# Last steps of a down projection as seven products, and the loads and sums around them moved

## The chip, the cores and the metric

The kernel runs on one core of one Trainium2 chip. The metric is device time in microseconds (us): the median of three runs is 2465.93 us, lowest 2465.27, highest 2466.05. A difference below 0.2% (4.9 us) is taken as no change.

## The reference, cut to what matters

One layer of an encoder: an input projection, two attention branches, an output projection, and then the feed-forward part, where the change lies. Sizes: 512 tokens, width 2048, inner width 5632, everything in float32.

```python
h2 = rmsnorm(x, norm_ffn)
u = h2 @ w_up                                   # 2048 -> 2 * 5632
u = up[:, :-2] * cw[0] + up[:, 1:-1] * cw[1] + up[:, 2:] * cw[2] + conv_b
gate, val = jnp.split(u, 2, axis=-1)
x = x + (jax.nn.silu(gate) * val) @ w_down      # 5632 -> 2048
```

## The kernel before, in words

Every float32 operand is split into two fp32r parts, hi (ScalarE, ACT, rounds it) and lo (VectorE, DVE, takes the rest), and a product is three matmuls: hi·hi, hi·lo, lo·hi.

The weights come in *units*: 256 input rows by 512 output columns. A unit is multiplied by 256 rows of activations of 512 tokens, so it is a two-by-two block product. In `products` this is done in Strassen–Winograd form: seven products, each on one sum or difference of blocks (a *form*), 7 x 2 x 3 = 42 matmuls of 128x256 a unit. In `tiles_by_halves` it is done plainly with eight: 48 such matmuls a unit. Here "seven products" and "plain" mean these two.

A `Product` unit goes through four phases. `load` (queue SP) fetches its four blocks to a tile `f` of seven places (four such tiles). `sums` (DVE) forms the three missing weight sums in `f`, in three additions. `prep` makes hi and lo of all seven forms in two pieces, "a" with four forms (1024 columns) and "b" with three (768): ACT casts to `wh`, DVE subtracts to `wl`. There are two buffers of each piece, so the prep of a unit waits until the unit two before it has been multiplied. Last comes the use on TensorE (PE). `advance` is called after each unit's matmuls and emits, for units ahead: prep of the next but one, sums of the one behind that, and load of the fourth. Some units are *kept*: their sums are made earlier in the program (`fetch`, `add`, `store`, called by `make_early`), kept in DRAM and loaded with the unit, so DVE does nothing for them at use.

When a step of `products` ends, `combine` turns its seven banks of PSUM (of eight) into four blocks. It comes in three pieces `one`, `two`, `three` that are handed to `advance` and stand between the pieces of the prep it emits. A plain step uses four banks and ends in `evac_plain`, four copies on ACT.

The feed-forward part is 22 steps `up(s)` of 8 units, then `down(part, n)`: three parts of the inner width (7, 7 and 8 units), each with four steps n = 0..3 over the output columns. I write (0,3) for part 0, n = 3, and U0, U1, ... for a step's units. Of the twelve, (0,0), (0,3) and (1,3) are plain before (table `PLAIN`). The activations of a part, made by `up` and kept in DRAM as `act`, must be loaded (`load_act`: 8 transfers of 128 KB per unit on SP, to slots of which there are 56) and split (`split_act`: a cast on ACT and a subtraction on DVE per tile) before the part's n = 0. They take the slots of the activations before them as these are used up. `before(i)` and `after(i)` are hooks around unit i of a step.

`keep` and `dma` pin instructions to the order of the code on their engine; a scheduler orders the rest, PE's matmuls among them, within the dependencies. The attention part ahead of the feed-forward part is mostly left to the scheduler.

## Time and profile before

| what | value |
|---|---|
| median of three runs | 2465.93 us |
| span of the profiled execution | 2464.1 us |
| PE busy | 2436.6 us, 99% |
| DVE busy | 1899.6 us, 77% |
| ACT busy | 1283.5 us, 52% |
| DMA | 525.45 MB, mean 213 GB/s |
| loads of kept sums | 88 of 512 KB |

The profiled execution's own time outside its span is not listed; the span is 1.8 us below the median of the runs, and the steps below are parts of the span. PE is busy throughout, so the time is PE's work plus the stretches in which it stands still or runs slowly. The steps can be told apart by counting weight loads: 42 or 48 for each unit, back from the last.

### The profile page before, as it was taken

How to read it: one execution, taken by the hardware profiler on the slowest of the kernel's cores; microseconds unless marked ns; L12 is line 12 of the kernel's file. 1: busy time of each engine (PE TensorE's matmuls, PEld its weight loads, DVE VectorE, ACT ScalarE, POOL GpSimd, SP SyncE). 2: the span in 40 equal slices, each digit the busy share in tenths (PEclk: the TensorE clock that was granted, in tenths of full speed). 3: DMA queues.
4: the chain of work that ended last, by engine and by line, in shares of the span. 5: the costliest groups of instructions: out<-in, count | busy, mean ns of one | idle time of the engine just before them, and what ended most of it. 6: DMA issues, size and time to landing. Idle time of an engine off the chain costs nothing.

```text
span 2464.1 us, 45745 instructions
## 1 busy us (share of the span) xinstructions
PE 2436.6 (99%) x17430; PEld 2276.2 (92%) x17430; DVE 1899.6 (77%) x3003; ACT 1283.5 (52%) x1962; POOL 330.5 (13%) x406
## 2 busy tenths in 40 slices
PE   9999999999999999999999999999999999999998
PEld 7888888888999888888999999999999999999998
DVE  6787667655888656557888888888888878696898
ACT  5354554365644322334666666666666666453633
POOL 1322122301000111111011111110111101000000
PEclk9999999999999999999999999999999999999999
DMA  5766766746655677777588888888888897766754
GB/s 197 257 230 213 234 207 230 238 139 205 197 163 175 200 271 245 237 232 245 166 213 230 224 225 224 218 234 222 224 228 218 234 277 187 218 187 176 221 158 131
DMA packets 340700, 525.45 MB, mean 213 GB/s; under 512 B 30720, under 2 KB 234112, under 8 KB 340480
## 3 DMA queue, kind: packets, MB, share of 16 engines
q1 hardware_dynamic: 254656, 319.68, 41.8%
q0 software_dynamic: 48384, 128.91, 21.8%
q10 hardware_dynamic: 37440, 73.94, 7.8%
q8 instruction: 136, 2.23, 0.4%
q14 instruction: 84, 0.69, 0.1%
HBM read 377.80 MB, written 98.57 MB: 193 GB/s over the span
## 4 chain that ended last, share of the span: by engine, by line
PE 94%; DVE 2%; DMA 1%; ACT 1%; issue 1%; SPq 0%; DVEq 0%; ACTq 0%
PE mm L78 91%; PE tr L78 2%; PE tr L503 1%; PE tr L351 0%; DVE wl L646 0%; DVE s L1076 0%; DMA a<-in_x_t 0%; DMA s<-act 0%; DMA f<-in_w_down 0%; ACT wh L645 0%; DVE u L795 0%; DVE s L687 0%; ACT s L1075 0%; DMA sums<-s 0%; DVE s L620 0%
## 5 line engine op out<-in xcount | busy, mean ns | idle before, releaser
L78 PE MATMUL mm<-s,wh 128*128 128x256 f32 (+1 forms) x9620 | 1725.0, 289 | 6.6 <-ACT wh L645 2.5
L78 PEld LDWEIGHTS mm<-s,wh 128*128 128x128 f32 x9620 | 1437.1, 188 | 48.7 <-ACT wh L645 3.1
L78 PE MATMUL mm<-s,wl 128*128 128x256 f32 (+1 forms) x4810 | 1249.9, 289 | 3.5 <-DVE wl L646 3.5
L78 PEld LDWEIGHTS mm<-s,wl 128*128 128x128 f32 x4810 | 851.0, 188 | 24.7 <-DVE wl L646 4.5
L645 ACT CAST wh<-f 128x1024 fp32r<-128x1024 f32 (+1 forms) x566 | 516.9, 942 | 482.5 <-PE mm L78 331.3
L646 DVE TENSOR_TENSOR wl<-f,wh 128x1024 fp32r<-128x1024 f32 (+1 forms) x566 | 601.8, 1088 | 147.7 <-ACT wh L645 146.3
L78 PE MATMUL mm<-hi,s 128*128 128x512 f32 x896 | 284.9, 394 | 5.7 <-ACT hi L163 5.7
L747 DVE TENSOR_TENSOR wl<-f,wh 128x1024 fp32r<-128x1024 f32 x85 | 104.1, 1224 | 165.4 <-ACT wh L746 159.7
L746 ACT CAST wh<-f 128x1024 fp32r<-128x1024 f32 x85 | 89.4, 1052 | 238.8 <-PE mm L78 207.0
L78 PEld LDWEIGHTS mm<-hi,s 128*128 128x128 f32 x896 | 167.6, 189 | 38.4 <-ACT hi L163 5.7
L163 ACT CAST hi<-raw 128x1024 fp32r<-128x1024 f32 (+1 forms) x97 | 100.9, 1040 | 188.5 <-PE mm L78 153.9
L78 PE MATMUL mm<-s,hi 128*128 128x512 f32 x640 | 195.4, 392 | 2.1 <-ACT o L519 1.6
L164 DVE TENSOR_TENSOR lo<-raw,hi 128x1024 fp32r<-128x1024 f32 (+1 forms) x97 | 117.5, 1211 | 102.8 <-ACT hi L163 98.7
L78 PE MATMUL mm<-lo,s 128*128 128x512 f32 x448 | 176.3, 395 | 0.0
L78 PEld LDWEIGHTS mm<-s,hi 128*128 128x128 f32 x640 | 119.2, 188 | 25.9 <-ACT o L519 1.8
L600 DVE TENSOR_TENSOR f<-f 128x512 f32<-128x512 f32 x195 | 133.5, 685 | 0.0
L1045 POOL DMA_DIRECT2D o<-a x44 | 52.9, 1202 | 557.8 <-ACT a L1044 336.9
L78 PE MATMUL mm<-s,lo 128*128 128x512 f32 x320 | 118.8, 391 | 0.0
L620 DVE TENSOR_TENSOR s<-s 128x256 f32<-128x256 f32 x236 | 93.2, 419 | 17.1 <-DMA s<-in_w_up 15.0
L78 PEld LDWEIGHTS mm<-lo,s 128*128 128x128 f32 x448 | 84.4, 188 | 16.6
L1042 ACT ACTIVATE o<-u,smalls 128x512 f32<-128x512 f32 x88 | 71.2, 809 | 33.3 <-DVE t L677 30.1
L603 DVE TENSOR_TENSOR f<-f 128x256 f32<-128x256 f32 x195 | 83.0, 426 | 6.7
(150 smaller groups left out, 2029.5 us busy)
## 6 DMA issues: line engine op xcount, KB each, us to landing
f<-sums SPq DMA_DIRECT2D x88, 512.0 KB, 5.3
f<-in_w_up SPq DMA_DIRECT2D x176, 256.0 KB, 3.8
o<-a POOLq DMA_DIRECT2D x88, 511.0 KB, 7.4
f<-in_w_up SPq DMA_DIRECT2D x281, 128.0 KB, 3.8
raw<-in_w_in SPq DMA_DIRECT2D x63, 512.0 KB, 4.4
sums<-s ACTq DMA_DIRECT2D x118, 256.0 KB, 4.1
s<-in_w_up POOLq DMA_DIRECT2D x86, 256.0 KB, 5.4
s<-act SPq DMA_DIRECT2D x168, 128.0 KB, 4.2
```

The source lines that it names most:

```text
L78: return nc.tensor.matmul(o, l, r, start=start, stop=stop, skip_group_check=True).ins
L163: nc.scalar.copy(hi[:, c:c + n], self.raw[:, c:c + n])
L164: nc.vector.tensor_tensor(lo[:, c:c + n], self.raw[:, c:c + n], hi[:, c:c + n].bitcast(F32), ALU.subtract)
L600: keep(nc.vector.tensor_tensor(f[:, 3:5], f[:, 2::-2], f[:, 6].unsqueeze(1).to_broadcast([P, 2, 256]), ALU.add))
L603: keep(nc.vector.tensor_tensor(f[:, 5], f[:, 4], f[:, 2], ALU.add))
L620: add = lambda *args: keep(nc.vector.tensor_tensor(*args, ALU.add))
L645: keep(nc.scalar.copy(hi, f))
L646: keep(nc.vector.tensor_tensor(lo, f, hi.bitcast(F32), ALU.subtract))
L746: keep(nc.scalar.copy(hi, self.f))
L747: keep(nc.vector.tensor_tensor(lo, self.f, hi.bitcast(F32), ALU.subtract))
L1042: keep(nc.scalar.activation(self.o[:, m], u[:, m], AF.Identity, bias=cb[:, i:i + 1], scale=cw[:, i, 1:2]))
L1045: keep(nc.gpsimd.dma_start(self.o[:, :, 1:], first[:, :, :S - 1], accum_op=ALU.add))
```

## The change

Five edits.

1. `PLAIN` goes: (0,3) and (1,3) are done with seven products; only (0,0) is plain.
2. The activations of parts 1 and 2 are loaded without block 1 (7 tiles, as in part 2 before), and the loads and splits are spread by two tables over (p,3) and the following n = 0: unit k of the new activations is loaded ahead of turn `LOADS[k]` and split behind turn `SPLITS[k]`, where turn 0 is U0 of (p,3) and turn 7 U0 of the next n = 0. For part 0 the loads in `up(21)` start two units later, and two of them move to (0,0).
3. Which units are kept: in `up(1)` to `up(20)` units 2 and 3 instead of 2, 3, 7; in n = 0 units 0 to 5 instead of 0 and 1; in (0,3) and (1,3) units 4, 5 and 6.
4. The order of the blocks in `f` is turned round, so that the second row block is loaded whole with one transfer (512 contiguous floats a row in `w_in` and `w_down`, two pieces of 256 in `w_up`); a unit that isn't kept takes two transfers instead of three.
5. The three additions of `sums` no longer follow each other: the first stands between the two pieces of the prep, the second behind them, and the third ahead of the next prep.

```diff
-PLAIN = ((0, 0), (0, 3), (1, 3))
+LOADS = 0, 2, 3, 5, 6, 8, 9, 11
+SPLITS = 2, 4, 5, 7, 8, 10, 11, 13
...
     def advance(*between):
-        prep_to(at["use"] + 1, between)
-        for phase, d in (("sums", 2), ("load", 4)):
+        def phase_units(phase, d):
             while at[phase] < len(products_) and products_[at[phase]].ready(phase, at["use"] + d):
-                getattr(products_[at[phase]], phase)()
                 at[phase] += 1
+                yield products_[at[phase] - 1]
+        hooks = [[*carried], [], []]
+        carried.clear()
+        for u in phase_units("sums", 2):
+            run_all(carried)
+            carried.clear()
+            ops = u.sums()
+            for place, op in zip((1, 2), ops):
+                hooks[place].append(op)
+            carried.extend(ops[2:])
+        for place, op in enumerate(between):
+            hooks[place].append(op)
+        prep_to(at["use"] + 1, hooks)
+        for u in phase_units("load", 4):
+            u.load()
         make_early()
...
         def load(self):
             f = self.f = ffn["f"].tile([P, 7, 256], F32, tag="f", name="f", bufs=4)
-            dma(f[:, 0:2], self.w[:, :, 0])
-            dma(f[:, 2], self.w[:, 1, 1])
+            dma(f[:, 0:2], self.w[:, 1])
             if self.made:
+                dma(f[:, 2], self.w[:, 0, 0])
                 dma(f[:, 3:], self.kept)
             else:
-                dma(f[:, 6], self.w[:, 0, 1])
+                dma(f[:, 2:4], self.w[:, 0])
...
-                    f[:, 3:5], f[:, 2::-2], f[:, 6].unsqueeze(1).to_broadcast([P, 2, 256]),
-                    ALU.add))
-                keep(nc.vector.tensor_tensor(f[:, 5], f[:, 4], f[:, 2], ALU.add))
-                keep(nc.vector.tensor_tensor(f[:, 6], f[:, 5], f[:, 1], ALU.add))
+            return [
+                lambda: add(f[:, 4:2:-1], f[:, 2:0:-1],
+                            f[:, 3].unsqueeze(1).to_broadcast([P, 2, 256])),
+                lambda: add(f[:, 5], f[:, 4], f[:, 1]),
+                lambda: add(f[:, 6], f[:, 5], f[:, 0])]
...
-            blocks = (0, 2, 7, 5, 4, 6, 3, 1)[:8 - (part == 2)]
+            blocks = (0, 2, 7, 5, 4, 6, 3, 1)[:8 - (part > 0)]
...
             if s == pairs_ff - 1:
-                load_act(0, i - 1)
+                load_act(0, i - 3)
...
-                 before=before, after=after, kept=(2, 3, 7) if s else range(8))
+                 before=before, after=after,
+                 kept={0: range(8), pairs_ff - 1: (2, 3, 7)}.get(s, (2, 3)))
...
+        def on_turn(work, turns, i):
+            turn = i if n else i + len(parts[part - 1])
+            if turn in turns and part + (n == 3) < 3:
+                work(part + (n == 3), turns.index(turn))
+
         def before(i):
-            if n == 0 and part:
-                load_act(part, 6 + i)
+            if n == part == 0:
+                load_act(0, 5 + i)
+            elif n in (0, 3):
+                on_turn(load_act, LOADS, i)
...
-            if part < 2 and n == 3:
-                load_act(part + 1, i - 1)
...
         def after(i):
-            if n == 0:
-                split_act(part, i + (5 if part else 2))
-            if part < 2 and n == 3:
-                split_act(part + 1, i - 2)
+            if n == part == 0:
+                split_act(0, i + 2)
+            elif n in (0, 3):
+                on_turn(split_act, SPLITS, i)
...
-        if (part, n) in PLAIN:
+        if part == n == 0:
...
-                     before=before, after=after, kept=(0, 1) if part and n == 0 else (),
+                     before=before, after=after,
+                     kept={0: range(6), 3: (4, 5, 6) if part < 2 else ()}.get(n, ()),
```

The instructions move at two places that matter here. The first is queue SP in `up(21)`, from its first activation load on (act_169 is unit 0 of part 0; f<-in_w_down of this shape is a unit of (0,0); sums_ are kept sums). Before:

```order
L75 DMA s<-act_169 128x256 x8
L75 DMA f<-in_w_up 128x2x256
L75 DMA f<-in_w_up 128x256 x2
L75 DMA s<-act_170 128x256 x8
L75 DMA f<-in_w_up 128x2x256
L75 DMA f<-in_w_up 128x256
L75 DMA f<-sums_261 128x1024
L75 DMA s<-act_171 128x256 x8
L75 DMA f<-in_w_down 128x2x512
L75 DMA s<-act_172 128x256 x8
L75 DMA f<-in_w_down 128x2x512
L75 DMA s<-act_173 128x256 x8
```

The same queue there in the changed kernel:

```order
L76 DMA f<-in_w_up 128x2x256 x7
L76 DMA f<-in_w_up 128x256
L76 DMA f<-sums_241 128x1024
L76 DMA s<-act_169 128x256 x8
L76 DMA f<-in_w_down 128x2x512
L76 DMA s<-act_170 128x256 x8
L76 DMA f<-in_w_down 128x2x512
L76 DMA s<-act_171 128x256 x8
L76 DMA f<-in_w_down 128x2x512
```

The first weights of (0,0) stood behind three units of activations and now stand behind one.

The second place is DVE at the end of (2,0), the last preps ahead of its `combine` (whose first addition writes u from mm and t). Before:

```order
L646 TENSOR_TENSOR wl<-f,wh 128x1024
L646 TENSOR_TENSOR wl<-f,wh 128x768
L600 TENSOR_TENSOR f<-f 128x512
L603 TENSOR_TENSOR f<-f 128x256
L604 TENSOR_TENSOR f<-f 128x256
L795 TENSOR_TENSOR u<-mm,t 128x2x256
```

In the changed kernel, from the prep of U0 of (2,1) on (s<-s is the split of activations):

```order
L668 TENSOR_TENSOR wl<-f,wh 128x1024
L622 TENSOR_TENSOR f<-f 128x2x256
L668 TENSOR_TENSOR wl<-f,wh 128x768
L622 TENSOR_TENSOR f<-f 128x256
L1097 TENSOR_TENSOR s<-s 128x256 x7
L622 TENSOR_TENSOR f<-f 128x256
L816 TENSOR_TENSOR u<-mm,t 128x2x256
```

The sums stand apart around the second `wl`, and a split of seven tiles, that of U7 of (2,0), now stands between the prep of the unit behind it and the `combine`; before, four more preps followed the last split.

## The prediction, on record before the run

> **What bounds the kernel now.** I read the page first, for the engine that carries the time.

> ```profile
> span 2464.1 us, 45745 instructions
> PE 2436.6 (99%) x17430; PEld 2276.2 (92%) x17430; DVE 1899.6 (77%) x3003; ACT 1283.5 (52%) x1962; POOL 330.5 (13%) x406
> PE 94%; DVE 2%; DMA 1%; ACT 1%; issue 1%; SPq 0%; DVEq 0%; ACTq 0%
> ```

> The chain of waits is 94% PE. So fewer matmuls shorten the time wherever PE is fed, and anything else counts only by the places where PE starves. To find those I cut the span at step boundaries and read the windows. The columns that matter are the length, the PEld count in its brackets (one weight load per matmul), DVE busy, and the last three: granted PE clock, DMA share, GB/s.

> ```profile
> 1600.00:1800.00 200.00, 200.00 (x1762) 200.00 (x1761) 174.77 (x228) 130.43 (x170) 25.24 (x21) 1.00 0.85 227
> 2007.40:2054.00 46.60, 42.84 (x335) 41.52 (x336) 40.42 (x82) 34.94 (x79) 5.97 (x5) 0.93 0.89 256
> 2012.40:2019.20 6.80, 6.11 (x28) 6.12 (x29) 6.31 (x10) 4.05 (x12) 0.00 (x0) 0.50 0.91 285
> 2054.00:2087.40 33.40, 33.40 (x296) 33.40 (x295) 27.99 (x41) 17.90 (x23) 1.76 (x2) 1.00 0.74 194
> 2120.80:2158.90 38.10, 38.10 (x338) 38.10 (x337) 23.16 (x43) 17.55 (x41) 1.72 (x2) 1.00 0.88 253
> 2158.90:2194.00 35.10, 33.95 (x296) 33.62 (x295) 33.41 (x64) 23.37 (x45) 1.72 (x2) 1.00 0.72 203
> 2299.10:2339.30 40.20, 38.78 (x339) 38.39 (x338) 37.93 (x72) 25.72 (x50) 1.72 (x2) 1.00 0.72 200
> 2339.30:2380.20 40.90, 38.73 (x339) 38.33 (x338) 37.78 (x57) 16.42 (x19) 2.21 (x4) 1.00 0.53 165
> 2380.20:2418.50 38.30, 38.30 (x339) 38.24 (x338) 35.23 (x53) 15.46 (x18) 2.16 (x4) 1.00 0.53 164
> ```

> The first row is five steps of `up` without a gap: 200 / 1761 = 0.1136 us per matmul, so 4.77 us for a seven-product unit and 5.45 for a plain one. The others are (0,0), a piece of it, (0,1), (0,3), (1,0), (2,0), (2,1) and (2,2). At that pace 336 matmuls take 38.2 us and 294 take 33.4. So (0,1), (0,3) and (2,2) run at PE's pace, while (0,0) loses 8.4 us, (1,0) 1.7, (2,0) 2.0 and (2,1) 2.7: 14.8 us in steps whose loads and splits the change moves.

> Next, why (0,0) loses. The waits of PE there, then ACT and SP in the timeline:

> ```profile
> PE mm L78 <- ACT t L799: 1.7, 1, 1.7
> PE mm L78 <- ACT s L1075: 1.5, 2, 1.2
> PE mm L78 <- DVE s L1076: 0.8, 2, 0.5
> ```

> ```profile
> 1995.39 0.40 SPq L75 DMA_DIRECT2D f<-in_w_down  x1
> 1995.88 9.41 SPq L75 DMA_DIRECT2D s<-act  x8
> 2005.39 0.45 SPq L75 DMA_DIRECT2D f<-in_w_down  x1
> ...
> 2004.78 1.05 ACT L746 CAST wh<-f 128x1024 fp32r<-128x1024 f32 x1 [4.64 <-DMA f<-in_w_down]
> 2006.98 2.53 ACT L1075 CAST s<-s 128x256 fp32r<-128x256 f32 x8
> 2011.50 1.04 ACT L746 CAST wh<-f 128x1024 fp32r<-128x1024 f32 x1 [2.00 <-DMA f<-in_w_down]
> 2012.45 0.58 ACT L799 COPY t<-mm 128x512 f32<-128x512 f32 x1
> ```

> SP sits 9.41 us over eight activation loads (they wait for slots of `up(21)`), and (0,0)'s second weights leave only behind them. ACT stands for 4.64 and 2.00 us waiting for weights; queued behind are the splits and the copy that frees a PSUM bank. PE starves for them, and then its clock falls to half for 6.8 us (29 matmuls in place of 60).

> **The change, part by part.**

> *Matmuls.* Fourteen units, 48 to 42: 84 x 0.1136 = **-9.5 us**. (0,3) runs at PE's pace in its row, so this is on the path in full.

> *What these units add off PE.* Per unit a second cast and subtraction, and sums where it isn't kept:

> ```profile
> L645 ACT CAST wh<-f 128x768 fp32r<-128x768 f32 x283 | 236.0, 834 | 145.5 <-PE mm L78 140.3 <-issue 3.3 <-DVE f L604 1.8
> L646 DVE TENSOR_TENSOR wl<-f,wh 128x768 fp32r<-128x768 f32 x283 | 269.8, 954 | 39.7 <-ACT wh L645 39.6
> ```

> What a DVE turn costs back to back I read in (1,0), where it never idles, and in (2,0) for seven tiles:

> ```profile
> 2173.79 2.09 DVE L646 TENSOR_TENSOR wl<-f,wh 128x1024 fp32r<-128x1024 f32 x2
> 2175.79 0.69 DVE L600 TENSOR_TENSOR f<-f 128x512 f32<-128x512 f32 x1
> ...
> 2177.32 2.77 DVE L1076 TENSOR_TENSOR s<-s 128x256 fp32r<-128x256 f32 x8
> 2180.00 2.08 DVE L646 TENSOR_TENSOR wl<-f,wh 128x1024 fp32r<-128x1024 f32 x2
> ...
> 2317.07 2.43 DVE L1076 TENSOR_TENSOR s<-s 128x256 fp32r<-128x256 f32 x7
> 2319.42 2.09 DVE L646 TENSOR_TENSOR wl<-f,wh 128x1024 fp32r<-128x1024 f32 x2
> ```

> Start to start: prep 2.0 us, sums 1.5, split 2.7 with eight tiles and 2.35 with seven. So before, a turn of (1,0) needed 2.0 + 1.5 + 2.7 = 6.2 us against PE's 4.77, several in a row. With the tables, turns 0 to 9 hold prep (2.0) and a split in every other or two of three (4.35 at most), no sums, since the units they would serve are kept; turn 6 has the `combine` (about 4.7) and no split. Only turns 10 and 11 exceed PE: 2.0 + 1.15 + 2.35 = 5.5 and 5.85, backlog 1.8 us; turn 12 (3.5) gives 1.3 back. In steady steps a turn's DVE work ends over 2 us ahead of its need, so (1,0) loses nothing: **-1.7**, and the added work in (0,3), whose DVE is busy 23.16 of 38.1, is covered. Lost cover would cost what (1,0) shows, 1.7 a part.

> *(2,0) and (2,1).* The same schedule removes their 2.0 + 2.7, but part 2 has an eighth unit. Its split (turn 13) stands behind the prep of unit 15, whose second cast may start only when PE has done with unit 13, so behind it nothing of U7's activations is ready when PE reaches U7. From these lengths:

> ```profile
> 2318.03 2.24 ACT L1075 CAST s<-s 128x256 fp32r<-128x256 f32 x7
> ```

> ACT needs 0.83 + 2.24 = 3.1 us for the cast and seven hi tiles. PE takes the seven hi·hi first (7 x 0.1136 = 0.8 us), so it idles at least 2.3 us; DVE's first lo comes at 3.0 to 3.8. I take a stall of **2.7**, new, in a place that had none. Net -4.7 + 2.7 = **-2.0** (from -4.7, if the scheduler's order hides it, to +1.4, if the clock then halves as at 2012, which cost 6.8 / 2 = 3.4 us).

> [...]

> *(0,0).* Activations start two units later, when their slots are free, and the weights stand one transfer group, not three, behind, so about 10 us earlier. ACT's 4.64 and 2.00 go, and with them the bank's wait and the half clock. What is late next is DVE:

> ```profile
> 2026.76 1.23 DVE L747 TENSOR_TENSOR wl<-f,wh 128x1024 fp32r<-128x1024 f32 x1 [0.39 <-ACT wh L746]
> 2027.90 1.22 DVE L1088 TENSOR_TENSOR o<-o 128x1024 f32<-128x1024 f32 x1
> 2086.99 0.68 DVE L795 TENSOR_TENSOR u<-mm,t 128x512 f32<-128x512 f32 x1
> 2092.48 1.22 DVE L795 TENSOR_TENSOR u<-t,u 128x1024 f32<-128x1024 f32 x1
> ```

> The `combine` (2086.99 to 2093.7, less the prep of 2.0 within it) is 4.7, a plain prep 1.1, a pass over a pair 1.2 (and one with `act`'s sums 2.7). From the end of `up(21)` on, DVE has combine, prep and split (8.5), then prep, pass and split (5.1), then prep, 2.7 and split (6.6), against 5.45 a unit. By count that ends U1's split 2.4 us into U1 and U3's 3.3 us into U3; the last lo tile is needed some 2 us in, so about 0.5 and 1.3 are lost. So (0,0) keeps 2.0 of its 8.4: **-6.4** (0 to -8.4).

> *`up` with one kept unit less.* +1.5 us of DVE in each of 20 steps. In the first row DVE is busy 174.77 / 200, so 33.4 of 38.2; it becomes 34.9, still under PE. Cost 0; if that cover fails, up to 20 x 1.5 = 30 us. Loads there shrink by 384 KB a step.

> *Sums apart.* DVE no longer waits 0.3 us a turn for ACT's second cast, off the path. But the first addition (0.69) now stands ahead of the `combine`'s second piece, which frees banks PE needs soon. In eight boundaries whose next units are not kept this is bounded by 0 and 8 x 0.69 = 5.5. A boundary of part 2 tolerates much:

> ```profile
> 2378.93 0.68 DVE L795 TENSOR_TENSOR u<-mm,t 128x512 f32<-128x512 f32 x1
> 2385.31 0.68 DVE L817 SCALAR_TENSOR_TENSOR t<-mm,t 128x512 f32<-128x512 f32 x1
> ```

> The last bank is read 5.8 us behind the boundary (2380.2) and (2,2) loses 0.1. I take **+1.0**, near the low end.

> *Longer rows; the rest of the order.* No PE wait in `up` or the gates is on these loads: 0. But other lengths make the scheduler order the attention part anew; its idle stretches come to some 5 us by this row and two alike, so ±4, taken 0:

> ```profile
> 495.00:511.00 16.00, 13.53 (x82) 11.12 (x80) 7.86 (x22) 10.23 (x29) 0.46 (x3) 1.00 0.39 142
> ```

> Sum: -9.5 - 1.7 - 2.0 - 6.4 + 1.0 = -18.6. The profiled span is 2464.1, 1.8 below the median of the runs; I subtract from the median, 2465.93: **2447.3 us**.

> **The rivals.**

> *Loads stay late.* The change asks for 8 x 128 KB + 512 KB (1.57 MB) every 4.77 us from SP alone, 330 GB/s, beside the convolution's and `act`'s transfers. Rows:

> ```profile
> 1985.00:1995.00 10.00, 10.00 (x90) 10.00 (x90) 8.94 (x13) 8.68 (x12) 2.40 (x2) 1.00 0.96 302
> 2025.00:2035.00 10.00, 9.50 (x84) 9.30 (x83) 9.50 (x20) 6.58 (x13) 0.00 (x0) 1.00 0.99 339
> ```

> At share 1 it moves 300 to 340, so the loads fall behind through `up(21)` and (0,0) keeps its stall: 2465.9 - 9.5 - 1.7 - 2.0 + 1.0 = 2453.7. Against it: the first weights have some 15 us of slack. [...]

> *New stalls eat part 2's gain.* The clock halves behind U7's stall (+3.4) and the boundaries pay in full (5.5 instead of 1.0): 2447.3 + 3.4 + 4.5 = 2455.2.

> *DVE becomes the bound of `up`* (the other side). If the 1.5 us lands on PE at each boundary, 2447.3 + 30 = 2477. It is slower than before from 18.6 / 20 = 0.93 us a step on. Against it: 3.3 us of DVE idle remain per step; for it: DVE is behind through half a step after each `combine`.

> *Nothing new waits*: all 14.8 us go and boundaries cost 0: 2465.9 - 9.5 - 14.8 = 2441.6, and a luckier attention order makes 2438.

> That the change doesn't do what it says, with kept sums not made in time, can't be here: it needs 85 early units, and 88 loads of kept sums are on the page.

> **How the numbers follow.** My forecast 52% (own range 2442 to 2453), loads late 18%, new stalls 14%, nothing waits 10%, DVE the bound 6%. The range leaves out DVE the bound and the far ends of the others: 2439 to 2458. No change is within 4.9 us (0.2%, what a measurement here can tell): faster means under 2461. All cases but DVE the bound lie there, less their tails: faster 0.90, same 0.05, slower 0.05.

> **What would show it.** 17430 - 84 weight loads; (0,3) and (1,3) at 33.4 us; (0,0) near 40 with the clock at 1.00 and ACT waiting for no weights; (1,0) at 33.4; one PE wait of 2 to 3 us on ACT's split at U7 of (2,0), none behind it; `up` still 38.2 a step. I am wrong if `up` takes longer, if (0,0) still shows half clock, or if PE waits for `mm` banks at boundaries.

## The result: slower by 0.6%

The changed kernel takes 2482.83 us (median of four runs, 2476.43 to 2484.57), the kernel before, run beside it, 2465.99 us (four runs, 2465.27 to 2467.52). The ratio is 1.0062, 95% interval 1.0048 to 1.0075. I had forecast 2447.3.

### The profile page after: what moved, and what is told of

Its sections match the earlier page's. It is cut to its first block, busy times and chain, and to the rows that moved or that the text cites. A ratio compares the mean times of both kernels' runs of the same rounds, so it can differ in the third digit from the quotient of the medians.

```text
span 2482.7 us, 45448 instructions
## 1 busy us (share of the span) xinstructions
PE 2441.7 (98%) x17346; PEld 2275.5 (92%) x17346; DVE 1905.1 (77%) x3061; ACT 1291.3 (52%) x1967; POOL 323.6 (13%) x400
## 3 DMA queue, kind: packets, MB, share of 16 engines
q1 hardware_dynamic: 227664, 317.57, 40.2%
q8 instruction: 135, 2.21, 0.4%
## 5 line engine op out<-in xcount | busy, mean ns | idle before, releaser
L79 PE MATMUL mm<-s,wh 128*128 128x256 f32 (+1 forms) x9564 | 1707.1, 290 | 17.5 <-ACT wh L667 6.9
L79 PEld LDWEIGHTS mm<-s,wh 128*128 128x128 f32 x9564 | 1415.3, 189 | 61.6 <-ACT wh L667 8.5
L79 PE MATMUL mm<-s,wl 128*128 128x256 f32 (+1 forms) x4782 | 1204.9, 289 | 1.4 <-DVE wl L668 1.4
L79 PEld LDWEIGHTS mm<-s,wl 128*128 128x128 f32 x4782 | 829.3, 188 | 21.9 <-DVE wl L668 2.0
L667 ACT CAST wh<-f 128x1024 fp32r<-128x1024 f32 x594 | 548.7, 942 | 531.4 <-PE mm L79 378.6
L668 DVE TENSOR_TENSOR wl<-f,wh 128x1024 fp32r<-128x1024 f32 x594 | 644.1, 1087 | 174.6 <-ACT wh L667 173.6
L622 DVE TENSOR_TENSOR f<-f 128x256 f32<-128x256 f32 (+1 forms) x636 | 323.7, 509 | 10.0 <-DMA f<-in_w_down 4.7
L79 PEld LDWEIGHTS mm<-hi,s 128*128 128x128 f32 x896 | 168.6, 190 | 39.5 <-ACT hi L163 6.2
L769 DVE TENSOR_TENSOR wl<-f,wh 128x1024 fp32r<-128x1024 f32 x71 | 86.9, 1224 | 132.4 <-ACT wh L768 129.2
L768 ACT CAST wh<-f 128x1024 fp32r<-128x1024 f32 x71 | 74.7, 1052 | 194.7 <-PE mm L79 166.6
L1066 POOL DMA_DIRECT2D o<-a x44 | 52.9, 1202 | 596.7 <-ACT a L1065 497.2
L79 PEld LDWEIGHTS mm<-lo,s 128*128 128x128 f32 x448 | 85.2, 190 | 21.0 <-DVE lo L164 4.3
L1074 POOL DMA_DIRECT2D o<-a x44 | 52.8, 1201 | 171.1 <-ACT a L1072 163.9
```

What stands on the lines that cost most here:

```text
L79: return nc.tensor.matmul(o, l, r, start=start, stop=stop, skip_group_check=True).ins
L622: add = lambda *args: keep(nc.vector.tensor_tensor(*args, ALU.add))
L667: keep(nc.scalar.copy(hi, f))
L668: keep(nc.vector.tensor_tensor(lo, f, hi.bitcast(F32), ALU.subtract))
L768: keep(nc.scalar.copy(hi, self.f))
L769: keep(nc.vector.tensor_tensor(lo, self.f, hi.bitcast(F32), ALU.subtract))
```

## The profile after

The page of the changed kernel, its first lines and the line of its DMA packets:

```profile
span 2482.7 us, 45448 instructions
PE 2441.7 (98%) x17346; PEld 2275.5 (92%) x17346; DVE 1905.1 (77%) x3061; ACT 1291.3 (52%) x1967; POOL 323.6 (13%) x400
DMA packets 312362, 520.17 MB, mean 210 GB/s; under 512 B 27472, under 2 KB 184272, under 8 KB 312144
```

PE has 84 weight loads fewer, as the change says, and yet is busy 5 us longer in a span 18.6 us longer (the medians differ by 16.8). So the question is not the matmuls. I cut the span at the same step boundaries as before and measured each step:

| step | before, us | after, us | difference | forecast |
|---|---|---|---|---|
| all ahead of up(0) | 1166.3 | 1180.8 | +14.5 | 0 |
| up(0) to up(20) | 802.3 | 803.3 | +1.0 | 0 |
| up(21) and (0,0) | 38.7 + 46.7 | 42.5 + 49.1 | +6.1 | -6.4 |
| (0,3), (1,3) | 38.1 each | 33.4 each | -4.6 each | -4.76 each |
| (1,0) | 35.1 | 37.0 | +1.9 | -1.7 |
| (2,0) | 40.2 | 47.0 | +6.9 | -2.0 with (2,1) |
| (2,1) | 40.9 | 38.2 | -2.8 | |

The windows of these steps, in the columns explained with the prediction: length, PE, PEld, DVE, ACT, POOL busy, granted clock, DMA share, GB/s. First all ahead of up(0), called the attention part below, then up(10), up(21), (0,0), (0,3), (1,0), (2,0), (2,1):

```profile
0.00:1180.80 1180.80, 1163.49 (x6216) 1001.69 (x6217) 788.15 (x1434) 522.66 (x880) 195.56 (x283) 0.99 0.63 211
...
1563.70:1601.90 38.20, 38.20 (x338) 38.20 (x338) 33.75 (x48) 24.50 (x33) 4.89 (x5) 1.00 0.82 215
...
1984.00:2026.50 42.50, 40.09 (x339) 39.89 (x338) 30.25 (x41) 24.37 (x35) 5.25 (x5) 0.96 0.92 251
2026.50:2075.60 49.10, 42.48 (x339) 41.30 (x338) 39.18 (x79) 33.78 (x75) 4.80 (x4) 0.93 0.90 253
...
2142.50:2175.90 33.40, 33.40 (x296) 33.40 (x295) 28.36 (x47) 20.19 (x39) 1.72 (x2) 1.00 0.91 273
2175.90:2212.90 37.00, 34.66 (x296) 33.85 (x295) 30.10 (x55) 21.78 (x44) 1.72 (x2) 1.00 0.88 272
...
2313.50:2360.60 47.10, 43.03 (x339) 41.63 (x339) 39.72 (x73) 26.46 (x54) 1.72 (x2) 0.93 0.88 273
2360.60:2398.70 38.10, 38.10 (x338) 38.10 (x337) 34.37 (x52) 16.88 (x19) 2.19 (x4) 1.00 0.51 163
```

(0,3) is what I forecast: PE never stands, DVE 28.36 of 33.4. But its DMA share is 0.91 (0.88 before), and that of (1,0) and (2,0) 0.88, where it was 0.72 before. The change filled the DMA queues just where it took cover away.

The clock is the second thing to see. These windows are the stretches at half clock; before, there was one, the 6.80 us in (0,0) (both kernels have another in their last 5 us, left out here):

```profile
287.20:290.60 3.40, 3.40 (x9) 2.64 (x9) 2.25 (x3) 1.97 (x4) 0.00 (x0) 0.51 0.92 268
587.60:594.40 6.80, 5.69 (x14) 4.33 (x15) 0.00 (x0) 1.02 (x1) 1.44 (x2) 0.50 0.54 174
638.80:642.20 3.40, 3.40 (x18) 3.40 (x17) 3.29 (x4) 2.20 (x3) 0.56 (x1) 0.50 0.57 175
2011.00:2014.40 3.40, 3.40 (x18) 3.40 (x17) 3.10 (x5) 3.40 (x6) 0.28 (x2) 0.50 1.02 278
2055.30:2062.10 6.80, 5.34 (x25) 5.34 (x26) 4.00 (x9) 6.80 (x15) 1.20 (x1) 0.50 1.06 331
2352.30:2359.10 6.80, 6.20 (x27) 5.91 (x28) 5.40 (x13) 2.67 (x8) 0.00 (x0) 0.50 0.66 234
```

They add up to 30.6 us, so at most 15.3 lost (13.7 if only PE's busy 27.4 us count), against 3.4 before. Some 11 to 12 us of what this execution lost are thus the price of the clock behind the waits, not the waits themselves. That price varies: the four timed executions had a granted clock of 0.993, 0.993, 0.994 and 0.997 and took 2484.57, 2484.30, 2481.36 and 2476.43 us. The profiled one is the first.

## The experiments

Unless said otherwise each is timed beside the kernel before on the same chip, whose median there was 2465.8 to 2466.6. Steps are read from each run's one profile. A step that an edit does not touch repeats to 0.1 us there ((2,0) is 40.2 in the kernel before, r2 and r14); up(21) with (0,0), where half clock falls differently, repeats to 0.8.

**r1: the early fetch of the attention part with its old rows.** The early fetches of the first part (two slots each) take column halves again, as before the change, with the four additions that go with them (not shown); all else is the changed kernel.

```diff
-                keep(nc.gpsimd.dma_start(x, self.w[:, b]))
+                keep(nc.gpsimd.dma_start(x, self.w[:, :, b] if self.by_cols else self.w[:, b]))
```

> The changed kernel with one thing undone: the early fetches in the attention part read two 256-wide pieces a row again, as before the change (sums added from them in the old order), which brings back the old order of instructions on PE, DVE and ACT there. Theory 'order': the attention part loses its 14.5 us because the scheduler ordered it anew; up(0) starts at 1166 us again instead of 1181, and the total is 2482.8 - 14.5, about 2468. Rival: the 14.5 us come from the kept units or the loads of the gates, which stay changed: up(0) still starts near 1181 and the total stays near 2483.

2471.84 us, ratio 1.0022 (1.0012 to 1.0032). up(0) starts at 1166.6, where it started before:

```profile
0.00:1166.60 1166.60, 1155.55 (x6215) 997.89 (x6216) 790.71 (x1434) 523.75 (x880) 191.07 (x283) 1.00 0.65 214
```

**r2: the opposite, the kernel before with only those rows made long.** The additions change with them here too. Of ACT's 881 rows in the attention part 877 then follow each other as in the changed kernel, and 707 as before (by operation, names and shapes).

```diff
-                keep(nc.gpsimd.dma_start(x, self.w[:, :, h]))
+                keep(nc.gpsimd.dma_start(x, self.w[:, h] if self.by_rows else self.w[:, :, h]))
```

> The kernel before with one thing added: the early fetches in the attention part read whole rows of 512, as in the change. Theory 'order': up(0) starts near 1181 and the total is 2466 + 14.5, about 2480. Rival (these fetches don't matter): up(0) at 1166, total 2466.

2476.52 us, ratio 1.0038 (1.0025 to 1.0050); up(0) starts at 1179.5, 13.2 us late, and nothing behind it moves by more than 0.8. The part before the change, and in this run:

```profile
0.00:1166.30 1166.30, 1154.68 (x6216) 997.25 (x6217) 798.84 (x1446) 522.39 (x880) 202.40 (x289) 1.00 0.66 216
...
0.00:1179.50 1179.50, 1161.36 (x6215) 1001.17 (x6216) 796.50 (x1446) 521.03 (x880) 202.24 (x289) 1.00 0.65 214
```

The two runs agree: this edit, which I costed at nothing, is worth 13 to 14 us in the profiled executions, which for the changed kernel and for r2 are the slowest of those timed; by the medians it is 10 to 11. PE's waits in the attention part, before and then after, the longest of each list (us in total, times, longest):

```profile
PE mm L78 <- ACT hi L163: 5.7, 1, 5.7
PE tr L78 <- ACT ph L507: 2.3, 3, 1.2
PE mm L78 <- ACT wh L645: 1.3, 1, 1.3
```

```profile
PE mm L79 <- ACT hi L163: 5.7, 2, 5.5
PE mm L79 <- DVE lo L164: 2.9, 2, 2.4
PE mm L79 <- ACT wh L667: 2.6, 1, 2.6
PE tr L79 <- DVE pl L528: 1.8, 3, 0.9
```

None of these releasers is a transfer, nor is any in the rest of the two lists. From the two attention windows, PE stands 1180.8 - 1163.5 = 17.3 us against 1166.3 - 1154.7 = 11.6 before (5.7 more), and three half-clock stretches of 13.6 us lose up to 6.8 more; that is some 12.5 of the 14.5. Matched by the number of the matmul, the changed kernel falls behind in two places, from 260 to 300 us (by 6.5) and from 540 to 627 us (by 6.5), and not at all from 650 us on; r2 falls behind mostly in the same two.

**r14: the early work of the attention part begins one unit later**, in the kernel before. No row is longer. I meant it as another order of that part.

```diff
-    windows.append((9, len(units)))
+    windows.append((10, len(units)))
```

> The kernel before, with the early fetches and sums beginning one row of units later (10 for 9): no row gets longer and no transfer is added, but the scheduler writes 654 of 893 DVE rows and 534 of 665 ACT rows of the attention part in another order. Theory 'any new order of that part costs, since the old one was a lucky one': up(0) starts 5 us or more later than 1166.3, total over 2471. Rival 'the loss came from the longer rows themselves, or from what that one order did': up(0) starts within 3 us, total within 2463 to 2470.

2465.75 us, ratio 0.9998 (0.9989 to 1.0008); up(0) starts at 1166.6:

```profile
0.00:1166.60 1166.60, 1155.31 (x6215) 997.55 (x6216) 797.65 (x1442) 522.33 (x880) 200.53 (x287) 1.00 0.66 215
```

But the run does not test what I meant it to. In the traces ACT's 881 rows follow each other exactly as before, DVE's too but for four additions that are gone (1446 rows, then 1442), and all but two of PE's 6216 matmuls, each within 0.6 us of its old start. How the count in the expectation came about the traces don't show. So it stays open whether any new order of this part would cost as much, what in this one costs the 13 us, and whether the longer rows add to it: row shape, additions and order come together in every kernel I ran.

**r3: part 0's activations on their old turns**, on top of r1.

```diff
             if s == pairs_ff - 1:
-                load_act(0, i - 3)
+                load_act(0, i - 1)
...
-            if n == part == 0:
-                load_act(0, 5 + i)
-            elif n in (0, 3):
+            if n in (0, 3) and not n == part == 0:
```

> As r1_att_order, and the activation loads of part 0 at their old turns in up(21). Theory 'full queues': moved two units later, these loads meet the first weights of (0,0) and the stores of act when the DMA engines are full, and the split of U5 comes late; undone, up(21) and (0,0) together take 85.4 us as before instead of 91.6, and the total is 6 us below r1. Rival: the order of sums and splits on DVE starves (0,0): 91.6 stays.

2465.41 us, ratio 0.9994 (0.9985 to 1.0003). up(21) and (0,0) together take 85.7 us, against r1's 90.2 and before's 85.4:

```profile
1969.70:2008.90 39.20, 38.60 (x340) 38.34 (x338) 28.88 (x38) 22.78 (x31) 4.01 (x5) 1.00 1.01 281
2008.90:2055.40 46.50, 42.72 (x335) 41.29 (x336) 40.27 (x82) 35.05 (x79) 5.95 (x5) 0.93 0.91 257
```

So the edit that should have gained 6.4 cost 4.5 here. How it costs is in the changed kernel's SP and ACT timelines (start, length, instruction; in brackets the idle time before it and what ended that):

```profile
2000.57 6.75 SPq L76 DMA_DIRECT2D s<-act  x8
...
2009.06 6.00 SPq L76 DMA_DIRECT2D s<-act  x8
...
2015.68 8.49 SPq L76 DMA_DIRECT2D s<-act  x8
...
2024.77 6.51 SPq L76 DMA_DIRECT2D s<-act  x8
```

```profile
2005.91 0.98 ACTq L1115 DMA_DIRECT2D act<-t  x2
2006.93 0.82 ACT L1063 ACTIVATE o<-u,smalls 128x512 f32<-128x512 f32 x1 [3.75 <-DMA act<-o]
...
2009.58 1.76 ACT L667 CAST wh<-f 128x1024 fp32r<-128x1024 f32 x2
...
2051.79 0.34 ACTq L1115 DMA_DIRECT2D act<-o  x1
2052.22 1.41 ACTq L1115 DMA_DIRECT2D act<-t  x2
2053.68 0.81 ACT L1063 ACTIVATE o<-u,smalls 128x512 f32<-128x512 f32 x1 [6.28 <-issue]
...
2056.32 2.53 ACT L1096 CAST s<-s 128x256 fp32r<-128x256 f32 x8
```

```profile
PE mm L79 <- ACT wh L667: 2.4, 1, 2.4
PE mm L79 <- ACT s L1096: 4.3, 2, 4.1
```

Begun two units later, a group of eight still takes 6 to 8.5 us. The slots were only a part of what it waited for: over the 32 us from the first such load on, SP's waits for a matmul to free a slot fall from 8.1 to 5.9 us, and its waits for other loads rise from 7.5 to 11.5, at a DMA share of 1.05 (0.98 before). The activation stores that `up` makes stand in ACT's own queue. ACT idles 3.75 us there until two of them have left, the cast of the next weights waits behind them, and PE 2.4 us for that. In (0,0) the last stores leave ACT only at 2052; behind them is U4's split at 2056.32, for which PE stands 4.1 us and then runs 6.8 us at half clock. The stores themselves were held by loads: the trace has a semaphore event of one of SP's loads at 2005.89, 2006.54 and 2051.69, and a store leaves at 2005.91, 2006.56 and 2051.79.

**r4: the sums together again**, three additions behind the prep, on top of r1.

```diff
-            ops = u.sums()
-            for place, op in zip((1, 2), ops):
-                hooks[place].append(op)
-            carried.extend(ops[2:])
+            run_all(u.sums())
```

> As r1_att_order, and the three sums of a unit follow each other behind the prep again. Theory 'a sum in the way': the first sum waits for weights that have not landed, between the two halves of an earlier unit's prep, and holds up that unit and the splits behind; undone, (1,0) falls from 37.0 to about 35 and (2,0) from 47.0 to about 43, and the total by 5 us or so. Rival: the loads themselves are late, wherever the sums stand: (1,0) and (2,0) stay within 1 us of 37.0 and 47.0.

2469.86 us, ratio 1.0026 (1.0003 to 1.0049; one of the ten executions, at a granted clock of 0.945, took 2496.69 and widens it). (1,0) 36.0 (r1 38.2), (2,0) 46.3 (47.8), up(9) and up(17) back at 38.2; up(21) is 3.1 shorter and (0,0) 3.7 longer. So the sums apart cost some 2 us in (1,0), 1.5 in (2,0) and 1.5 to 2 in `up` here (in r11 and r13 the sign in (1,0) is the other); most of (2,0)'s loss is something else.

**r5: fewer kept units in n = 0**, on top of r3: U0 and U1 in (1,0) and (2,0).

```diff
-                     kept={0: range(6), 3: (4, 5, 6) if part < 2 else ()}.get(n, ()),
+                     kept={0: (0, 1) if part else (), 3: (4, 5, 6) if part < 2 else ()}.get(n, ()),
```

> The kernel of the third run (attention order and part 0's loads as before the change), with fewer kept units in n = 0: none in (0,0), units 0 and 1 in (1,0) and (2,0), as before the change; load and split tables stay. Each kept unit that goes takes 384 KB off the loads, 1.2 us at the 320 GB/s seen there, and gives DVE 1.5 us of sums back. Theory 'the loads of kept sums fill the queues': four units in (2,0) free 4.9 us, so (2,0) falls from 47.6 to 41 to 43 and (1,0) from 37.2 to about 36; total near 2459. Rival 'DVE is what is late, by sums and splits between the preps': four more sums, 6 us of DVE, in (2,0): it stays at 47 to 50, (1,0) 38 to 40; total 2465 to 2470.

2464.09 us, ratio 0.9987 (0.9977 to 0.9997). (1,0) 37.2 to 35.7, (2,0) 47.6 to 46.1: 1.5 each, between the two expectations. (2,0) in this run:

```profile
2293.00:2339.10 46.10, 43.27 (x339) 41.32 (x338) 44.24 (x85) 26.41 (x54) 1.72 (x2) 0.96 0.87 254
```

DVE is now busy 44.24 of 46.10. With the kept sums it was 39.72 of 47.10 and stood waiting for loads, as these rows of the changed kernel, ACT's and DVE's, show:

```profile
2331.31 1.78 ACT L667 CAST wh<-f 128x1024 fp32r<-128x1024 f32 x2 [1.84 <-DMA f<-sums]
```

```profile
2337.43 0.69 DVE L622 TENSOR_TENSOR f<-f 128x512 f32<-128x512 f32 x1 [1.58 <-DMA f<-in_w_down]
...
2353.32 0.69 DVE L622 TENSOR_TENSOR f<-f 128x512 f32<-128x512 f32 x1 [0.90 <-DMA f<-in_w_down]
```

The three waits for loads are 1.84 us of ACT's and 2.48 of the 7.4 us in which DVE stands. A kept unit only hands 1.5 us of DVE on to 1.2 us of DMA (an estimate: 384 KB at 320 GB/s, between the 245 and 346 that r3 moved in parts of (2,0) at a DMA share of 1.0), and both are short there.

**r6 and r7: the old turns for parts 1 and 2**, on top of r3, with the new kept units (r6) and with r5's (r7).

```diff
-            if n in (0, 3) and not n == part == 0:
-                on_turn(load_act, LOADS, i)
+            if n == 0 and part:
+                load_act(part, 6 + i)
+            if part < 2 and n == 3:
+                load_act(part + 1, i - 1)
...
-            elif n in (0, 3):
-                on_turn(split_act, SPLITS, i)
+            elif n == 0:
+                split_act(part, i + 5)
+            elif n == 3 and part < 2:
+                split_act(part + 1, i - 2)
```

> The kernel of the third run with the activations of parts 1 and 2 loaded and split on the turns they had before the change (seven tiles, and the new choice of kept units, stay). If the tables' spreading is what makes the loads of (2,0) meet the kept sums' loads, (2,0) goes to about 41 to 43, (1,0) to 35 to 36, while (2,1) goes back to about 40.9: total near 2461 to 2463. If the kept sums alone are the cause (loads of 512 KB whichever turn), (2,0) stays above 46 and the total is 2465 to 2469. (0,3) and (1,3), now with DVE's splits packed into them, stay 33.4 in both.

2479.56 us, ratio 1.0053 (1.0038 to 1.0068): (1,0) 47.6, (2,0) 51.5.

> Both of the last two together: old turns for loads and splits of parts 1 and 2, and the old kept units in n = 0. What is left of the change is the seven products in (0,3) and (1,3) with their three kept units, seven tiles, longer rows and the sums apart. Theory 'loads': (2,0) near 40 to 41, (2,1) near 40.9, (1,0) 35 to 36, so before less 9.3 plus 1 to 3: 2458 to 2460. Rival 'sums apart on DVE': (2,0) stays 4 us or more over its 40.2, total over 2462.

2471.69 us, ratio 1.0021 (1.0012 to 1.0031): (1,0) 41.8, (2,0) 47.4. The theory fails in both. r7's total is where its rival put it, over 2462, but r9, without the sums apart, has the same loss. The tables are not the harm: behind short steps the old turns are worse. So the harm had to be in the short steps themselves.

**r9: the seven products alone**, in the kernel before.

```diff
-PLAIN = ((0, 0), (0, 3), (1, 3))
+PLAIN = ((0, 0),)
```

> The kernel before with one edit: (0,3) and (1,3) as seven products (no kept units in them, all loads and splits on their old turns). My prediction's reckoning, matmuls on the path in full: 2466 - 9.3 = 2456.7, (0,3), (1,3) at 33.4 and the steps behind them unchanged. Theory 'the plain steps covered the splits and loads': the seven units add 7 x (0.95 + 1.5) = 17 us to DVE's 23.2 in (0,3), 40 against 33.4, so (0,3) or (1,0) and (1,3) or (2,0) get 5 us or more each back: 2466 to 2478.

2473.66 us, ratio 1.0029 (1.0018 to 1.0040), with 84 matmuls fewer. (0,3), (1,0) and (2,0):

```profile
2120.60:2155.30 34.70, 33.80 (x297) 33.60 (x297) 32.84 (x58) 20.54 (x41) 1.72 (x2) 1.00 0.80 222
2155.30:2198.00 42.70, 36.18 (x297) 35.40 (x296) 40.88 (x75) 25.19 (x50) 1.72 (x2) 0.96 0.76 216
2298.20:2346.20 48.00, 40.84 (x338) 39.10 (x338) 46.35 (x85) 26.34 (x53) 1.72 (x2) 1.00 0.78 226
```

(0,3) and (1,3) become 3.5 and 4.65 us shorter, (1,0) and (2,0) 7.6 and 7.8 longer. DVE is nearly full in all three, at DMA shares of 0.76 to 0.80: the plain step's slack (DVE 23.16 of 38.1 before) was where the next part's splits were made. Without it they are made in n = 0, on PE's time.

**r8: U7's load and split one turn earlier**, on top of r3, for the stall that I forecast there.

```diff
-LOADS = 0, 2, 3, 5, 6, 8, 9, 11
-SPLITS = 2, 4, 5, 7, 8, 10, 11, 13
+LOADS = 0, 2, 3, 5, 6, 8, 9, 10
+SPLITS = 2, 4, 5, 7, 8, 10, 11, 12
```

> The kernel of the third run with the last unit of activations (U7 of part 2, and by the same index the eighth turn only there) loaded one turn earlier (10 for 11) and split one turn earlier (12 for 13). My prediction's theory of a stall at U7 behind its late split: the wait of about 2.5 us in U7 and the half clock behind it go, (2,0) falls by 3 to 5 us, total near 2461. Rival 'the loads are late': the earlier load only makes the units ahead later, (2,0) stays within 1.5 us of 47.6, total 2464 to 2467.

2465.40 us, ratio 0.9997 (0.9988 to 1.0007). U7 of (2,0) falls from 9.18 to 5.35 us; a unit at PE's pace takes 4.76. So the stall is there, in its place and size. (2,0) takes 43.1 instead of 47.6, but U5 8.89 instead of 7.17, and (2,1) 40.7 instead of 38.2: a part of the delay only moved.

**r10: three of seven subtractions of each split on POOL**, on top of r5, to relieve DVE.

```diff
+POOL = 4, 5, 6
...
-                keep(nc.vector.tensor_tensor(
+                keep((nc.gpsimd if part and k in POOL else nc.vector).tensor_tensor(
```

> The kernel of r5 (few kept units) with three of seven subtractions in each split of parts 1 and 2 on POOL instead of DVE. DVE is busy 44.1 of 46.1 us in (2,0) there and its sums keep ACT waiting 8.4 us. Theory 'DVE is the bound of (2,0) once the kept sums go': 1 us less a split, five splits: (2,0) falls to 41 to 43, (1,0) to 34 to 35, total 2458 to 2461. Rival 'the loads' (DMA share 0.92 there): (2,0) stays at 45 to 47, total 2463 to 2465. A third, POOL slower than DVE by several times, so that the lo tiles come late: (2,0) over 47.

2473.73 us, ratio 1.0031 (1.0020 to 1.0043): (1,0) 47.6, (2,0) 48.2. The third theory holds. The subtractions on DVE from 2120 to 2345 us, which is most of (0,3) to (2,0), in r5 and here, and all of POOL's here:

```profile
L1105 DVE TENSOR_TENSOR s<-s 128x256 fp32r<-128x256 f32 x105 | 36.5, 418 | 0.0
```

```profile
L1106 DVE TENSOR_TENSOR s<-s 128x256 fp32r<-128x256 f32 x56 | 29.2, 583 | 0.0
```

```profile
L1106 POOL TENSOR_TENSOR s<-s 128x256 fp32r<-128x256 f32 x45 | 58.5, 1325 | 62.5 <-ACT s L1105 56.6 <-DMA s<-act 5.9
```

These means, 1325 on POOL and 583 beside it on DVE, mix two kinds. One by one, 37 of POOL's 45 take 0.72 to 0.98 us (0.72 to 0.74 where DVE stands), and DVE's take 0.41 to 0.43 as in r5 or, beside POOL's, 0.95 to 0.97. But three of POOL's take 3.6, 5.6 and 10.0 us, and beside them DVE runs row after row at its usual length. One of them is in this group of six:

```profile
2166.96 13.62 POOL L1106 TENSOR_TENSOR s<-s 128x256 fp32r<-128x256 f32 x6 [1.74 <-ACT s L1105]
```

In (1,0) PE waits for POOL, 5.2 us at the longest:

```profile
PE mm L80 <- POOL s L1106: 9.0, 2, 5.2
```

So this run doesn't tell whether DVE bounds (2,0): the lo tiles came late from POOL.

**r11: r5 with r4's and r8's edits.**

> The kernel of r5 with the sums together again (as in the fourth run) and U7's load and split a turn earlier (as in the eighth). If the gains add: (1,0) -1, (2,0) and (2,1) together -2 to -3, up17 -1: 2459 to 2461, faster than before by 0.2 to 0.3%. If DVE is full in (2,0) whatever the order, (2,0) stays near 46 and the total is 2463 to 2465.

2464.24 us, ratio 0.9994 (0.9984 to 1.0003). (1,0) 38.1, (2,0) 44.0, (2,1) 41.0: the gains don't add.

**r12: (1,3) plain again**, on top of r5, with part 2 on its old turns, part 1 in eight tiles, and U0 to U5 of (2,0) kept. Beside the diff of r6, for part 2 alone:

```diff
-        if part == n == 0:
+        if (part, n) in ((0, 0), (1, 3)):
...
+                     kept={(0, 3): (4, 5, 6), (1, 0): (0, 1), (2, 0): range(6)}.get((part, n), ()),
```

> The kernel of r5 with (1,3) plain again, part 2's activations loaded and split on their old turns, part 1 loaded with all eight tiles, and units 0 to 5 of (2,0) kept. Theory 'a plain step covers the next part's splits and loads': of the change's gain in parts 1 and 2 only (0,3)'s remains, (1,3) goes back to 38.1, but (2,0) falls to 38 to 40 and (2,1) to 38 to 39, so (1,3) to (2,1) take 115 to 117 against 118.6 in the changed kernel and 119.2 before; total 2459 to 2461. Rival 'the kept sums' loads are what makes (2,0) late, whatever (1,3) is': (2,0) stays at 44 or more, total 2466 or more.

2464.17 us, ratio 0.9994 (0.9985 to 1.0004). (1,3), (2,0) and (2,1):

```profile
2261.20:2299.30 38.10, 38.10 (x338) 38.10 (x337) 22.22 (x42) 16.32 (x37) 1.72 (x2) 1.00 0.89 263
...
2299.30:2338.00 38.70, 38.49 (x339) 38.29 (x338) 32.55 (x59) 27.20 (x51) 1.72 (x2) 1.00 0.88 267
2338.00:2376.40 38.40, 38.40 (x339) 38.27 (x338) 35.56 (x54) 16.10 (x18) 2.22 (x4) 1.00 0.56 173
```

The three take 115.2 us; 119.2 before and 118.6 in the changed kernel. The same loads of kept sums, at the same DMA share of 0.88, now cost 0.5 us at most, with most of the splits and of the activation loads done in (1,3). So (1,3) as seven products brings 4.6 us and its lost cover takes more: (2,0) and (2,1) together take 77.1 here, 84.3 in r5 and 85.2 in the changed kernel.

**r13: r12 with the sums together** (r4's diff).

> The kernel of r12 with the sums together behind the prep, as before the change. If the sums apart cost by what stands ahead of the combine and between the wl's, up(17) loses its 1 us and (1,0) up to 1.5: 1 to 3 us less than r12. If r11's (1,0) of 38.1 beside r5's 35.7 was due to the sums together, (1,0) is 2 us over r12's.

2465.30 us, ratio 0.9998 (0.9989 to 1.0008). up(9) and up(17) 38.2 again (39.0 and 38.8 in r12), but (1,0) 39.5 (38.0) and (2,1) 39.8 (38.4). The sums apart cost in `up` and gain in (1,0) and (2,1), about the same; the two totals can't be told apart.

**r15: the kept sums alone**, in the kernel before: U0 to U5 of (1,0) and (2,0) kept (before, the early units ran out at U0 of (1,0)), fewer in `up`.

```diff
-                 before=before, after=after, kept=(2, 3, 7) if s else range(8))
+                 kept=((2, 3, 7) if s % 2 and s < 21 else (2, 3)) if s else range(8))
...
-                     before=before, after=after, kept=(0, 1) if part and n == 0 else (),
+                     kept=range(6) if part and n == 0 else (),
```

> The kernel before with one edit: units 0 to 5 of (1,0) and (2,0) kept (before, U0 of (1,0) alone was), and in turn unit 7 no longer kept in eleven of the steps up(2) to up(21); (0,3) and (1,3) stay plain. It is the change's third edit without the seven products. Theory 'the plain steps cover, and DVE is late in n = 0': with 9 us fewer sums on DVE (1,0) falls from 35.1 to 33.4 to 34, (2,0) and (2,1) from 81.1 to 77, as in r12, up steps stay 38.2: 2459.5 to 2461.5, faster than before by 0.2% or a little more. Rival 'the kept sums' loads make n = 0 late by themselves': (1,0) and (2,0) grow by 1.5 us and more each, as r3 beside r5 showed: 2466 to 2470.

2466.93 us, ratio 1.0002 (0.9993 to 1.0011). (2,0) falls to 38.2, as expected, but (2,1) only to 40.3, and (1,0) rises to 36.1. The profiled execution is 2462.4 us, 4.5 below the median of the eleven runs (2462.2 to 2469.6); these executions go with the granted clock: the two at 0.999 took 2462.3 in the mean, the five at 0.998 2466.3, the four at 0.997 2468.1. I found no version that beats the kernel before by more than a measurement can tell.

## Why the prediction was wrong, point by point

*Matmuls, -9.5.* Right: (0,3) and (1,3) are 9.3 shorter.

*"Longer rows; the rest of the order ... ±4, taken 0".* The largest miss, +14.5. r1 and r2 show that the early fetch's row shape costs it, together with the additions and the order that come with it; PE waits there for ACT and DVE, and for no transfer. Which of the three costs it stays open (r14 did not separate them). The step that failed is the price: I bounded the risk by the attention part's existing idle time, and left out that new waits can bring stretches at half clock, up to 6.8 of the 14.5.

*"(0,0): about 10 us earlier ... -6.4".* It is +6.1 with up(21), a miss of 12.5. What I said of the weights came true: ACT's 6.6 us of waits for them are gone. What failed is "when their slots are free": slots were about half of what SP waited for, and starting later took 2.2 us off that half and added 4.0 to the waits for other loads (r3). The rival "loads stay late" named the mechanism and priced it as the old stall, with no gain. It left out who else stands in line: `up`'s stores in ACT's queue, ACT behind them, and up(21) itself, which had been free. r3 takes 4.5 of it back.

*"(1,0) loses nothing: -1.7" and "(2,0) and (2,1): -2.0".* +1.9 and +4.1. DVE's count was right for what it counted: busy 30.1 of 37.0 in (1,0), with no longer 6.2 us a turn. The step that failed is the overlap, which I counted for DVE alone. What that missed is that DVE's work had gone to the queues: 896 KB of weights instead of 512 KB in a kept unit, beside 896 KB of activations, at a share of 0.88 to 0.91. r5 and r9 show both ends: keep the sums and the loads are late; don't and DVE is full. "The added work in (0,3) ... is covered" was true of (0,3), whose price came due one step on (r9, r12). The prediction priced lost cover at 1.7 a part; r9 measures 7.6 and 7.8.

*U7's stall, 2.7, to +3.4 more if the clock halves.* Right in place and size (r3: 4.4 over the pace, 3.4 us of the unit being at half clock; r8 takes 3.8 of it back), but one delay of several: U5 and U6 were late already.

*`up`, 0.* +1.0, in up(9) and up(17), from the sums apart (gone in r4). The rival in which DVE bounds `up` needed 0.93 us a step; it was 0.05. *Boundaries, +1.0*: (0,1), (0,2), (1,1) and (1,2) changed by less than 0.2.

The sum of the misses, 14.5 + 12.5 + 3.6 + 6.1 + 1.0 - 1.0 = 36.7, is the distance from -18.6 to +18.6 but for 0.5. Only one of my rivals made the kernel slower, DVE as the bound of `up`; the loss came from elsewhere.

## What to carry to other kernels

A slower step that runs at its engine's pace can be the place where the next step's work is hidden: before shortening it, add up what DVE and the queues do in it and in the step behind it together, and only then call its time a gain. Moving work from an engine to the queues is not free where the queues are nearly full; yet r12 pays almost nothing at the share at which the changed kernel pays 8.9 us, so the share is a warning and not a price. A load that starts later has to be priced with everything else in the queues then, the stores of other engines included. Where a scheduler orders part of the program, compare that part too, even if the edit only changes the shape of a transfer, and compare which row follows which, not the places in the list (r14).
